# Attention with exponentials on two engines: a third exponential block for VectorE in the first and the third job, and two moved steps

## The chip, the cores and the metric

The kernel runs on one core of a Trainium2 chip. The core has a matrix engine (TensorE, PE in the profile), ScalarE (ACT), VectorE (DVE), GpSimd (POOL) and a queue engine for transfers (SyncE, SP). Each engine carries out its own instruction stream in order; semaphores tell one engine that another has finished something. The metric is the device time of one execution in microseconds. The kernel before takes 412.01 us, the median of three runs (411.99 to 412.39).

## The reference

Grouped-query attention with 8 batches, 512 positions, 32 query heads, 8 key/value heads and head width 64, all in float32:

```python
K_expanded = np.repeat(K, heads_per_group, axis=2)
V_expanded = np.repeat(V, heads_per_group, axis=2)
...
scores = np.einsum('bhqd,bhkd->bhqk', Q, K_expanded) * scale
weights = np.exp(scores - np.max(scores, axis=-1, keepdims=True))
weights = weights / (np.sum(weights, axis=-1, keepdims=True) + 1e-10)

output = np.einsum('bhqk,bhkd->bhqd', weights, V_expanded)
```

There is no mask. Four query heads share one key/value head.

## The kernel before

**Units and jobs.** A unit `u` is one batch and two key/value heads, so there are 32 units. A job `j` is one key/value head of a unit with its four query heads, so there are 64 jobs, and unit `u` has the jobs `2u` and `2u + 1`. A job's four heads form two pairs `i`. For each pair the scores are computed transposed, keys on the 128 partitions and the 512 queries along a row, in four chunks of keys `kc` and for the two heads `m` of the pair. One (i, kc, m) is a block of 128 x 512 scores, and a job has 16 of them.

**Two ways to take an exponential.** Most blocks go to ScalarE, two blocks (1024 columns) to an instruction: `act_tile` (L273) computes the scores on TensorE into a PSUM tile `s_ps` and takes the exponential into `pt` (L279). `s_ps` has two buffers. The first blocks of the second pair, `taken(j)` of them (L242), go another way, by a formula on the bits of a float16 number that VectorE and GpSimd share. `exp_d` (L283) computes their scores into a PSUM tile `d_ps` and scales them to an integer `u` on VectorE (L290). `exp_d2` (L297) takes the mantissa bits `f` on VectorE (L301), then `g` and the product `w` on GpSimd (L304, L308). `exp_d4` (L314) adds `u` and `w` into `pt` on VectorE (L317), and this runs in the middle of the job behind. `d_ps` has one buffer of two banks, each of 512 columns; the same tile name serves for the transposes of Q.

**How many blocks.** `WIDE` (L41) names the jobs in which `taken` is three: the even jobs from 4 on. In all others but the last it is two. With two, ScalarE has seven tiles of 1024 columns; with three, six and one of 512. In the loop, the 512-column tile of a wide job has its scores in the second bank of a `d_ps` tile (`beside`, L563), while the first bank takes a transposed Q. The functions `apart` (L195) and `trans_q(..., other=...)` (L202) tell the framework that two instructions touch different banks of one tile; where nothing is said, the framework makes the later one wait for the earlier one.

**The rest of a job.** `pv` (L333) multiplies the exponentials by the values, 32 matmuls for a pair in four groups of eight, into a PSUM tile with one buffer; a column of ones beside the values gives the sums. `norm` (L372) takes the reciprocal of the sums (L387) and multiplies (L393), and `store` writes a finished unit out through SP. `trans_q` turns a job's Q by TensorE (L210) and VectorE copies it to `qt` (L214). The keys of unit 0 and 1 are turned by TensorE as well (`first_keys` L172, `first_k` L147); those of later units by transposing transfers on SP (`dma_k` L185).

**The order of work** is written out by hand: the text of the kernel is the order of each engine's stream. A job of the loop (L521 to L585) issues its ScalarE tiles 0 to 6 one after the other and puts between them the values and the normalisation of the job before, the transposes of Q for a later job (two jobs ahead; up to job 2 the loop catches up), and the three steps of the other exponential. Near the end of job `j`, the third block of job `j + 1`, where that is a wide one, is computed into the second bank of the `d_ps` tile (L579). Job 0 is written out in front of the loop (L502 to L518).

**Loads.** GpSimd's queue issues the loads of Q, K and V, which also convert to bfloat16. Job 0 and 1 use the Q of unit 0, job 2 and 3 that of unit 1, job 4 and 5 that of unit 2 ("the third unit"). Units 2 and 3 are loaded at the start of job 1, behind a one-element copy `gate` (L528) that waits for ScalarE's fourth tile of job 0, so that these loads stay behind the first ones.

Of the kernel before, what the change touches and what calls it, by code (L numbers as in the profile page):

```python
# [37 lines left out]
LAST_SUMS = NLAST * 2 * 4  # L38


WIDE = lambda j: j >= 4 and j % 2 == 0  # L41


@with_exitstack
# [23 lines left out]
def fast_path(ctx, tc, Q, K, V, out, flag, ident):  # L68
    nc = tc.nc
# [3 lines left out]
    SC = S // 128  # L73
# [26 lines left out]
    gate = const_pool.tile([1, 1], FP16, name="gate")  # L100
# [31 lines left out]
    def load_q(u, lo=0, hi=2 * HPG):  # L132
        b, gp = divmod(u, GP)
        h0 = gp * 2 * HPG
        if u not in qn:
            qn[u] = qnat_pool.tile([128, SC, 2 * HPG, D], BF16, name="q_nat")
        nc.gpsimd.dma_start(  # L137
            out=qn[u][:, :, lo:hi, :],
            in_=Q[b, :, h0 + lo:h0 + hi, :].rearrange("(sc p) h d -> p sc h d", p=128),
        )  # L140

    def d_tile():
        return d_pool.tile([128, 2, S], FP32, name="d_ps")
# [51 lines left out]
    def apart(this, other):  # L195
        if other is not None:
            tc.declare_no_dep(
                this.ins, other.ins, reason="the two are in different banks of one tile"
            )
        return this  # L200

    def trans_q(j, bank, lo=0, hi=NPAIR, other=None):  # L202
        u, g = divmod(j, 2)
        ps = bank.bitcast(BF16).rearrange("p (i sc c) -> p i sc c", i=NPAIR, sc=SC)
        done = []
        for i in range(lo, hi):
            for sc in range(SC):
                h = g * HPG + 2 * i
                done.append(apart(
                    nc.tensor.transpose(ps[:, i, sc, :], qn[u][:, sc, h:h + 2, :], ident), other  # L210
                ))
        if u not in qt:
            qt[u] = qt_pool.tile([128, 2, NPAIR, S], BF16, name="qt")
        return done, lambda: apart(nc.vector.tensor_copy(  # L214
            out=qt[u][:, g, lo:hi, :], in_=ps[:, lo:hi, :, :].rearrange("p i sc c -> p i (sc c)")
        ), other)
# [3 lines left out]
    def piece(bank, done, read):  # L220
        copy = read()
        for other, written, taken_out in pieces:
            if other != bank:
                for this in done:
                    apart(this, taken_out)
                for before in written:
                    apart(copy, before)
        pieces.append((bank, done, copy))
# [13 lines left out]
    def taken(j):  # L242
        return 1 if j == NJOB - 1 else 3 if WIDE(j) else 2

    def d_block(j):
        return SC * 2 - 2 if j == NJOB - 1 else 0

    def act_tiles(j):
        every = [(i, kc, m) for i in range(NPAIR) for kc in range(SC) for m in range(2)]
        first = DPAIR * SC * 2 + d_block(j)  # L250
        mine = [n for n in range(len(every)) if not first <= n < first + taken(j)]
        groups = [[n for n in mine if n // 2 == h] for h in range(len(every) // 2)]
        return [[every[n] for n in group] for group in groups if group]

    jobs, osb, invs = {}, {}, {}
# [17 lines left out]
    def act_tile(j, n, spare=None):  # L273
        group = act_tiles(j)[n]
        i, kc, lo = group[0]
        ps = s_pool.tile([128, 2, S], FP32, name="s_ps") if spare is None else spare
        for _, _, m in group:
            scores(j, ps[:, m, :], i, kc, m)
        return nc.scalar.activation(  # L279
            out=jobs[j]["pt"][:, i, kc, lo:, :], in_=ps[:, lo:, :], func=EXP, scale=scale  # L280
        )

    def exp_d(j, lo, hi, ps, other=None):  # L283
        st = jobs.setdefault(j, {})
        if "u" not in st:
            for name, dtype in (("u", I16), ("f", I16), ("g", BF16), ("w", BF16)):
                st[name] = dve_pool.tile([128, 3, S], dtype, name=name + "16")[:, 0:taken(j), :]
        for n in range(lo, hi):
            apart(scores(j, ps[:, n - lo, :], DPAIR, *divmod(d_block(j) + n, 2)), other)
        return lambda: nc.vector.tensor_scalar(  # L290
            out=st["u"][:, lo:hi, :], in0=ps[:, 0:hi - lo, :], scalar1=A_U, scalar2=B_U,
            op0=ALU.mult, op1=ALU.add,
        )
# [3 lines left out]
    def exp_d2(j, engine=None):  # L297
        st = jobs[j]
        by_bits = engine is None
        engine = engine or nc.gpsimd  # L300
        nc.vector.tensor_single_scalar(  # L301
            out=st["f"], in_=st["u"], scalar=1023, op=ALU.bitwise_and
        )
        engine.tensor_scalar(  # L304
            out=st["g"], in0=st["f"], scalar1=-EXP_F1, scalar2=EXP_K * 2.0 ** (24 * by_bits),
            op0=ALU.add, op1=ALU.mult,
        )
        product = lambda: engine.tensor_tensor(  # L308
            out=st["w"], in0=st["g"], in1=st["f"].bitcast(FP16) if by_bits else st["f"],
            op=ALU.mult,  # L310
        )
        return product() if by_bits else product
# [20 lines left out]
    def pv(j, i, lo, hi):  # L333
        st = jobs[j]
        u, g = divmod(j, 2)
        b, gp = divmod(u, GP)
        if lo == 0:

            t = d_tile() if (j, i) == (NJOB - 1, 0) else pv_tile()
            t = t.rearrange("p m (qc c) -> p m qc c", qc=SC)  # L340
            st["pv"][i] = t[:, :, :, 0:D + 1]
        order = blocks(j, i)
        for n in range(lo, hi):
            kc, m, qc = order[n]
            nc.tensor.matmul(  # L345
                st["pv"][i][:, m, qc, :],
                st["pt"][:, i, kc, m, qc * 128:(qc + 1) * 128],
                vt[b % 2][:, kc, 2 * gp + g, :],
                start=(n < 2 * SC and qc == 0),
                stop=(n >= len(order) - 2 * SC and qc == SC - 1),  # L350
            )
# [136 lines left out]
    bank = pv_tile()  # L488
# [20 lines left out]
    exp_d(0, 0, 2, d_tile())()  # L509
    act_tile(0, 3)  # L510
    act_tile(0, 4)
    exp_d2(0)
    bank = pv_tile()
    piece(0, *trans_q(1, bank[:, 0, :], 0, 1))
    act_tile(0, 5)
    piece(1, *first_keys(1, bank[:, 1, 0:S // 2]))
    act_tile(0, 6)
# [3 lines left out]
    for j in range(1, NJOB - 1):  # L521
        last = j - 1
        u, g = divmod(j, 2)
        b, gp = divmod(u, GP)
        open_job(j)
        if j == 1:

            nc.gpsimd.tensor_copy(out=gate, in_=jobs[0]["pt"][0:1, 0, SC - 1, 0, 0:1])  # L528
            load_q(2)
            load_q(3)  # L530
        if g == 0 and u >= 1 and u + 3 < NU:
            load_q(u + 3)
        if (gp, g) == (1, 0) and b + 1 < B:
            load_k(b + 1)
        if 3 <= 2 * gp + g < 3 + SC and b + 1 < B:
            load_v(b + 1, chunks=(2 * gp + g - 3,))
        if j == 1:
            dma_k(0, 2)
        if gp == 2 and g == 0 and b + 1 < B:
            dma_k(b + 1)  # L540

        cut = (4, 18) if taken(j) > 2 else (11, 19)
        act_tile(j, 0)
        if j == 1:
            piece(1, *first_k(1, 0, bank[:, 1, S // 2:]))
        exp_d(j, 0, 2, d_tile())()
        act_tile(j, 1)

        if j == 8:
            check_v(0, 0)  # L550
        if g == 1 and 1 < j and b < B - 1:
            check_v(b, gp)
        if 0 <= j - 8 * (B - 1) < SC:
            check_v(B - 1, j - 8 * (B - 1))
        pv(last, 0, 0, 16)
        act_tile(j, 2)
        pv(last, 0, 16, 32)
        norm(last, 0)
        act_tile(j, 3)

        reads = []
        bank = d_tile()
        beside = act_tile(j, 4, bank) if taken(j) > 2 else None  # L563

        ahead = (j + 1,) if j < 2 else (3, 4) if j == 2 else (j + 2,)
        for n, to in enumerate(ahead):
            if to < NJOB:
                reads.append(trans_q(to, bank[:, n, :], other=beside)[1])
        if j == 1:
            reads.append(first_k(1, 1, bank[:, 1, :])[1])  # L570
        exp_d4(last)
        check_sums()
        exp_d2(j)
        copies = [read() for read in reads]
        if taken(j) == 2:
            act_tile(j, 4)
        pv(last, 1, 0, cut[0])
        act_tile(j, 5)
        if taken(j + 1) > 2:  # L579
            exp_d(j + 1, 2, taken(j + 1), bank[:, 1:2, :], copies[0])()  # L580
        pv(last, 1, *cut)
        act_tile(j, 6)
        pv(last, 1, cut[1], 32)
        norm(last, 1)
        del jobs[last]  # L585

    j, last = NJOB - 1, NJOB - 2
# [144 lines left out]
```

## Time and profile before

| what | before |
|---|---|
| median of three runs | 412.01 us (411.99 to 412.39) |
| the profiled execution | 412.64 us, its span 410.9 us |
| ScalarE busy | 401.3 us, 98% |
| TensorE busy | 377.8 us, 92% |
| VectorE busy | 342.7 us, 83% |
| GpSimd busy | 306.0 us, 74% |
| granted TensorE clock | 0.998 |

The span reaches from the first to the last instruction; the time of an execution is about 1.7 us longer. In the rows of the profile, a line such as `L279 ACT ACTIVATE pt<-s_ps 128x1024 ... x419 | 396.7, 1298 | 0.6 <-PE s_ps L261 0.6` names the line of the kernel, engine and operation, output and input with their shapes, how often it ran, the time it was busy and the mean length of one in nanoseconds, and the idle time of the engine in front of it with what ended most of it. In a timeline a row gives start and length in microseconds, and equal instructions that follow each other are one row with their number.

### The profile page before, as it was taken

The numbers are of one execution on the slowest core, as the hardware profiler recorded it, in microseconds if no ns is written. First come the engines' busy times: TensorE is split into PE (matmuls) and PEld (weight loads), VectorE is DVE, ScalarE is ACT, GpSimd is POOL, SyncE is SP. The second block draws the span as 40 slices with busy tenths as digits, with TensorE's granted clock in tenths as the row PEclk, the third lists the DMA queues.
The fourth block names the chain that finished last, engine by engine and source line by source line (L and its number), as shares of the span: only waits on it lengthen the run. The fifth ranks groups of instructions, "written<-read, shape, count | busy, mean of one in ns | idle before, by whom it ended". The sixth has DMA issues, their size and how long they took to land.

```text
span 410.9 us, 13048 instructions
## 1 busy us (share of the span) xinstructions
PE 377.8 (92%) x5666; PEld 232.9 (57%) x5666; DVE 342.7 (83%) x609; ACT 401.3 (98%) x454; POOL 306.0 (74%) x216
## 2 busy tenths in 40 slices
PE   7999999999999999999999999999999999999985
PEld 3565565555555555555655655555555655655553
DVE  4787898888888888888888888888889888998775
ACT  5999999999999999999999999999999999999995
POOL 9868767888679777688777897587776887676562
PEclk9999999999999999999999999999999999999999
DMA  9999974999739996499994999669986799742205
GB/s 152 159 244 165 210 148 135 195 140 219 168 107 229 134 230 157 110 203 114 194 270 77 201 185 218 155 86 221 189 176 155 133 202 197 158 138 104 104 30 183
DMA packets 93294, 67.74 MB, mean 165 GB/s; under 512 B 53296, under 2 KB 76336, under 8 KB 93232
## 3 DMA queue, kind: packets, MB, share of 16 engines
q0 software_dynamic: 55488, 24.91, 52.9%
q1 hardware_dynamic: 36688, 41.56, 36.3%
q8 instruction: 45, 0.74, 0.8%
q10 hardware_dynamic: 1056, 0.39, 0.4%
q14 instruction: 17, 0.14, 0.1%
HBM read 50.33 MB, written 33.55 MB: 204 GB/s over the span
## 4 chain that ended last, share of the span: by engine, by line
ACT 86%; PE 8%; DVE 3%; issue 1%; ACTq 0%; POOL 0%; DVEq 0%
ACT pt L279 86%; PE s_ps L261 5%; PE pv L345 2%; DVE o_sb L393 1%; PE s_ps L476 1%; DVE pt L317 1%; DVE qt L214 0%; DVE u L290 0%; ACTq L279 0%; DVE ok L356 0%; DVE inv_last L387 0%; PE pv L493 0%; PE d_ps L345 0%; DVE inv L387 0%; DVE f L301 0%
## 5 line engine op out<-in xcount | busy, mean ns | idle before, releaser
L279 ACT ACTIVATE pt<-s_ps 128x1024 f16<-128x1024 f32 x419 | 396.7, 1298 | 0.6 <-PE s_ps L261 0.6
L345 PEld LDWEIGHTS <-pt 128*128 128x128 f16 x4096 | 142.2, 98 | 75.7 <-issue 55.6
L345 PE MATMUL pv<-v,pt 128*128 128x65 bf16 x4064 | 179.3, 195 | 0.9 <-DVE o_sb L393 0.7
L261 PE MATMUL s_ps<-qt,kt 64*128 64x512 bf16 x781 | 153.1, 383 | 23.7 <-ACT pt L279 17.2
L308 POOL TENSOR_TENSOR w<-g,f 128x1024 bf16<-128x1024 bf16 (+1 forms) x63 | 163.0, 2587 | 5.3
L304 POOL TENSOR_SCALAR g<-f 128x1024 bf16<-128x1024 int16 (+1 forms) x63 | 78.4, 1245 | 90.9 <-DVE f L301 90.8
L290 DVE TENSOR_SCALAR u<-d_ps 128x1024 int16<-128x1024 f32 (+1 forms) x94 | 97.7, 1039 | 0.5 <-PE d_ps L261 0.5
L261 PEld LDWEIGHTS <-kt 64*128 64x128 bf16 x960 | 55.3, 93 | 66.6 <-issue 37.1
L393 DVE TENSOR_TENSOR o_sb<-pv,inv 128x512 f32<-128x512 f32 x121 | 83.7, 692 | 4.2
L387 DVE RECIPROCAL inv<-pv 128x8 f32<-128x8 f32 x121 | 25.1, 207 | 49.9 <-PE pv L345 49.9
L317 DVE TENSOR_TENSOR pt<-u,w 128x1536 uint16<-128x1536 int16 (+1 forms) x64 | 51.4, 803 | 0.3 <-POOL w L308 0.2
L261 PE MATMUL d_ps<-qt,kt 64*128 64x512 bf16 x179 | 46.0, 375 | 0.1
L214 DVE COPY qt<-d_ps 128x1024 bf16<-128x1024 bf16 x62 | 42.3, 684 | 0.0
L210 PEld LDWEIGHTS <-q_nat 128*128 128x128 bf16 x508 | 28.5, 98 | 20.2 <-issue 20.2
L210 PE MATMUL d_ps<-ident,q_nat 128*128 128x128 bf16 x496 | 38.3, 220 | 0.0
L301 DVE TENSOR_SCALAR f<-u 128x1536 int16<-128x1536 int16 (+1 forms) x64 | 31.2, 487 | 0.0
L122 POOL DMA_DIRECT2D v<-in_V_dram x32 | 29.1, 911 | 0.0
L137 POOL DMA_DIRECT2D q_nat<-in_Q_dram x33 | 27.1, 821 | 0.1
L279 ACT ACTIVATE pt<-d_ps 128x512 f16<-128x512 f32 x30 | 26.8, 894 | 0.0
L232 DVE TENSOR_REDUCE okv<-v 128x1 f32<-128x512 bf16 x32 | 21.6, 676 | 0.0
L261 PE MATMUL s_ps<-qt,kt_first 64*128 64x512 bf16 x56 | 11.1, 386 | 2.5 <-ACT pt L279 2.2
L261 PEld LDWEIGHTS <-kt_first 64*128 64x128 bf16 x64 | 4.1, 93 | 6.1 <-issue 3.7
(54 smaller groups left out, 46.2 us busy)
## 6 DMA issues: line engine op xcount, KB each, us to landing
out_dram<-o_sb SPq DMA_DIRECT2D x31, 1024.0 KB, 7.3
q_nat<-in_Q_dram POOLq DMA_DIRECT2D x31, 512.0 KB, 6.3
k_nat<-in_K_dram POOLq DMA_DIRECT2D x7, 512.0 KB, 8.5
v<-in_V_dram POOLq DMA_DIRECT2D x28, 128.0 KB, 7.0
kt<-kt SPq DMA_DIRECT2D x14, 256.0 KB, 4.5
out_dram<-o_sb SPq DMA_DIRECT2D x3, 256.0 KB, 2.3
kt<-k_nat SPq DMA_TRANSPOSE x32, 6.1
v<-in_V_dram POOLq DMA_DIRECT2D x4, 96.0 KB, 8.0
```

The source lines that it names most:

```text
L122: nc.gpsimd.dma_start(out=vt[b % 2][:, sc, lo:hi, 0:D], in_=V[b, sc * 128:(sc + 1) * 128, lo:hi, :],)
L210: nc.tensor.transpose(ps[:, i, sc, :], qn[u][:, sc, h:h + 2, :], ident), other
L214: return done, lambda: apart(nc.vector.tensor_copy(out=qt[u][:, g, lo:hi, :], in_=ps[:, lo:hi, :, :].rearrange("p i sc c -> p i (sc c)")), ...
L261: return nc.tensor.matmul(ps, keys[64 * m:64 * m + 64, g if u == 0 else g ^ m, kc * 128:(kc + 1) * 128], qt[u][64 * m:64 * m + 64, g, i, : ...
L279: return nc.scalar.activation(out=jobs[j]["pt"][:, i, kc, lo:, :], in_=ps[:, lo:, :], func=EXP, scale=scale)
L290: return lambda: nc.vector.tensor_scalar(out=st["u"][:, lo:hi, :], in0=ps[:, 0:hi - lo, :], scalar1=A_U, scalar2=B_U, op0=ALU.mult, op1=AL ...
L301: nc.vector.tensor_single_scalar(out=st["f"], in_=st["u"], scalar=1023, op=ALU.bitwise_and)
L304: engine.tensor_scalar(out=st["g"], in0=st["f"], scalar1=-EXP_F1, scalar2=EXP_K * 2.0 ** (24 * by_bits), op0=ALU.add, op1=ALU.mult,)
L308: product = lambda: engine.tensor_tensor(out=st["w"], in0=st["g"], in1=st["f"].bitcast(FP16) if by_bits else st["f"], op=ALU.mult,)
L317: nc.vector.tensor_tensor(out=st["pt"][:, DPAIR, :, :, :].rearrange("p kc m q -> p (kc m) q")[:, d_block(j):d_block(j) + n, :].bitcast(U16 ...
L345: nc.tensor.matmul(st["pv"][i][:, m, qc, :], st["pt"][:, i, kc, m, qc * 128:(qc + 1) * 128], vt[b % 2][:, kc, 2 * gp + g, :], start=(n < 2 ...
L393: nc.vector.tensor_tensor(out=osb[u][:, lo:hi, h:h + 2, :].rearrange("p qc m d -> p m qc d"), in0=sums[:, :, lo:hi, 0:D], in1=inv[:, :, lo ...
```

## The change

`WIDE` holds for all even jobs, so jobs 0 and 2 hand three blocks to VectorE and GpSimd instead of two. Job 0 takes its third block's scores into a `d_ps` tile of its own behind ScalarE's fifth tile, and `exp_d2` of job 0 comes one transposing step later. The gate and the load of the third Q unit move in front of it. Job 2's third block is computed at the end of job 1, behind ScalarE's last tile instead of in front of the values, where the loop does it for later jobs. Job 2, now a wide one, uses the second `d_ps` bank for its 512-column tile; so the Q of job 4, which was turned in that bank together with the Q of job 3, is turned there later, behind ScalarE's tile 5.

```diff
-WIDE = lambda j: j >= 4 and j % 2 == 0
+WIDE = lambda j: j % 2 == 0
...
     act_tile(0, 4)
-    exp_d2(0)
+    exp_d(0, 2, taken(0), d_tile())()
+    nc.gpsimd.tensor_copy(out=gate, in_=jobs[0]["pt"][0:1, 0, SC - 1, 0, 0:1])
+    load_q(2)
     bank = pv_tile()
     piece(0, *trans_q(1, bank[:, 0, :], 0, 1))
+    exp_d2(0)
     act_tile(0, 5)
...
         if j == 1:
-
-            nc.gpsimd.tensor_copy(out=gate, in_=jobs[0]["pt"][0:1, 0, SC - 1, 0, 0:1])
-            load_q(2)
             load_q(3)
...
-        ahead = (j + 1,) if j < 2 else (3, 4) if j == 2 else (j + 2,)
+        ahead = (j + 1,) if j < 3 else (j + 2,)
...
         act_tile(j, 5)
-        if taken(j + 1) > 2:
+        if j == 2:
+            trans_q(4, bank[:, 1, :])[1]()
+        if taken(j + 1) > 2 and j > 1:
             exp_d(j + 1, 2, taken(j + 1), bank[:, 1:2, :], copies[0])()
         pv(last, 1, *cut)
         act_tile(j, 6)
+        if j == 1:
+            exp_d(2, 2, taken(2), bank[:, 1:2, :], copies[0])()
         pv(last, 1, cut[1], 32)
```

## The prediction

> **What bounds the kernel now.** I read the page first: the busy shares, the chain that ended last, the costliest groups.
>
> ```profile
> span 410.9 us, 13048 instructions
> PE 377.8 (92%) x5666; PEld 232.9 (57%) x5666; DVE 342.7 (83%) x609; ACT 401.3 (98%) x454; POOL 306.0 (74%) x216
> ...
> ACT 86%; PE 8%; DVE 3%; issue 1%; ACTq 0%; POOL 0%; DVEq 0%
> ...
> L279 ACT ACTIVATE pt<-s_ps 128x1024 f16<-128x1024 f32 x419 | 396.7, 1298 | 0.6 <-PE s_ps L261 0.6
> ```
>
> ScalarE is busy 98% and its exponentials idle 0.6 us in all, so every microsecond taken off ScalarE shows, and every wait put on it shows too. The mean of 1298 ns is not the price of a tile, because neighbours overlap. The price is the distance between ends, which the timeline of ScalarE gives (start, length, instruction):
>
> ```profile
> 6.59 29.56 ACT L279 ACTIVATE pt<-s_ps 128x1024 f16<-128x1024 f32 x32 [0.58 <-PE s_ps L261]
> 35.88 0.77 ACT L279 ACTIVATE pt<-d_ps 128x512 f16<-128x512 f32 x1
> 36.36 12.22 ACT L279 ACTIVATE pt<-s_ps 128x1024 f16<-128x1024 f32 x13
> ```
>
> Ends are at 36.15, 36.65 and 48.58: a 512-column tile costs 0.49, and a 1024-column one (48.58 - 36.65) / 13 = 0.917. The first tile, from idle, takes 1.03; 1.03 + 31 x 0.917 = 29.46, so the 32 tiles contain only 0.10 us of waiting. Next the timelines of VectorE and GpSimd, where the added work goes:
>
> ```profile
> 8.45 1.23 DVE L290 TENSOR_SCALAR u<-d_ps 128x1024 int16<-128x1024 f32 x1 [0.48 <-PE d_ps L261]
> 9.71 0.85 DVE L301 TENSOR_SCALAR f<-u 128x1024 int16<-128x1024 int16 x1
> 10.48 0.40 DVE L214 COPY qt<-pv 128x512 bf16<-128x512 bf16 x1
> ...
> 15.96 0.68 DVE L317 TENSOR_TENSOR pt<-u,w 128x1024 uint16<-128x1024 int16 x1
> 16.56 0.42 DVE L301 TENSOR_SCALAR f<-u 128x1024 int16<-128x1024 int16 x1
> 16.90 0.68 DVE L214 COPY qt<-d_ps 128x1024 bf16<-128x1024 bf16 x1
> 17.50 0.41 DVE L160 COPY kt_first<-d_ps 128x512 bf16<-128x512 bf16 x1
> ...
> 21.56 0.21 DVE L387 RECIPROCAL inv<-pv 128x8 f32<-128x8 f32 x1 [0.80 <-PE pv L345]
> ...
> 23.34 1.28 DVE L214 COPY qt<-d_ps 128x1024 bf16<-128x1024 bf16 x2
> ```
>
> ```profile
> 8.65 1.66 POOL L122 DMA_DIRECT2D v<-in_V_dram  x2
> ...
> 36.58 1.47 POOL L304 TENSOR_SCALAR g<-f 128x1536 bf16<-128x1536 int16 x1 [1.66 <-DVE f L301]
> 38.14 3.10 POOL L308 TENSOR_TENSOR w<-g,f 128x1536 bf16<-128x1536 bf16 x1
> ```
>
> See that VectorE's rows of job 1 (15.96 to 17.91) stand without gaps, and that a three-block `f` at 35.94 to 36.49 (0.55) has its `w` only at 41.24, 4.75 later. TensorE in job 2:
>
> ```profile
> 20.85 0.67 PE L345 MATMUL pv<-v,pt 128*128 128x65 bf16 x16
> 21.45 0.39 PE L261 MATMUL s_ps<-qt,kt_first 64*128 64x512 bf16 x2
> 21.77 1.07 PE L210 MATMUL d_ps<-ident,q_nat 128*128 128x128 bf16 x16
> 22.77 0.39 PE L261 MATMUL s_ps<-qt,kt_first 64*128 64x512 bf16 x2
> ```
>
> **The change part by part.** Jobs count from 0, (2,6) is tile 6 of job 2, times are the trace's own clock. Durations by shape are those of the steady state (`u` 1.22 for two blocks and 0.68 for one, `f` 0.42 and 0.55, exp_d4 0.68 and 0.95 for two and three blocks). Small gaps come from neighbouring rows: ScalarE or VectorE to TensorE 0.05, TensorE to either 0.04, `f` to `g` 0.09, `w` to exp_d4 0.03; queued VectorE work starts 0.08 before its predecessor's end.
>
> *Two blocks leave ScalarE* (jobs 0 and 2): 2 x (0.917 - 0.49) = -0.85.
>
> *Job 0's short tile takes an s_ps buffer.* In later wide jobs it sits in d_ps; here the tile behind it needs the buffer of (0,3), which is read until 6.59 + 1.03 + 3 x 0.917 = 10.37. Scores 10.42 to 10.81, exponential from 10.85, 1.03 from idle: end 11.88. Without the wait 10.37 + 0.49 + 0.917 = 11.78. +0.10. Job 0 ends at 12.79 instead of 13.12.
>
> *Job 0's third block, and what is queued behind it.* d_ps has one buffer, so its scores wait for the first `u` (9.68): matmul 9.73 to 10.10, second `u` (0.68) to 10.82, job 1's Q copy to 11.15, `f` of three blocks 11.07 to 11.62. `w` ends 4.75 later, 16.37 (before: 14.05). exp_d4, 0.95 for three blocks, then ends at 17.35 (before: 16.64), where it had been waiting for nothing. Behind it stand job 1's `f` and the copies of job 2's Q and of the swapped keys, 1.27 in the rows (16.64 to 17.91): 18.62. Now the wait: the change puts job 2's third score block on TensorE behind (1,6), into the half of d_ps that the swapped-key copy reads. TensorE stands until 18.68. Queued behind are that matmul (0.31), 13 value matmuls (0.51) and only then (2,0): scores at 19.50, tile end 19.50 + 0.38 + 0.04 + 1.03 = 20.95. Unhindered it is 12.79 + 8 x 0.917 = 20.13. +0.82.
>
> *The Q load moved ahead of `g` on GpSimd.* Its issue (0.82, the mean of such rows) starts near 10.7, behind the memsets and the gate copy (0.18), and ends before `f` (11.62), so `g` loses nothing in the queue. But `f` may: in the trace `f` took 0.85 instead of 0.42 while GpSimd issued a DMA that had begun 0.25 earlier (9.46). An undisturbed 0.42 ending at 10.56 began at 10.14, 0.68 after that issue. The new `f` meets an issue 0.2 to 0.4 old: a delay of 0.28 to 0.48 by that row, zero if it slips in first. All of it passes down the chain above. I take 0.30, the row being nearly the same meeting; ends kept: 0 and 0.48. The trace does not show the other bound, a gain; none is possible, as `f` cannot start before its `u`.
> The Trainium skill ("SBUF — State Buffer", Who interferes with whom) says of VectorE and GpSimd that whoever issues first holds the shared ports for the whole instruction and the other is fully blocked. By that rule `f` would wait for the whole issue; the row above let it go at 0.68.
>
> *The third Q load in the other queues.* load_q(3) now stands behind the longer `w` (16.4 instead of 14.96), load_q(4) and load_k(1) behind job 1's `w` (about 1 later than 20.28 and 21.09). They are wanted in job 4 and after 30 us; median landing is 6.3 and 8.5. Covered, so 0. SP's queue is unchanged.
>
> *Job 4's Q transposed behind (2,5).* In the first place these eight transposes stood in one batch of 16 (21.77, 1.07), which caused the 0.10 of waiting: -0.10. In the new place no independence of the two banks is declared, and in the built order TensorE's first of them waits for VectorE's copy of job 3's Q, out of the other bank of the same tile. When does that copy end? (2,0)'s scores at 19.50 are followed by the first half of job 1's values, which wait for job 0's normalisation (one pv buffer): second `u` of job 2 from 19.09 to 19.77, reciprocal and product to 20.62. Values from 20.68, (2,2) at 21.28, second half 21.60 to 22.27, reciprocal 22.31. From reciprocal to the end of the first Q copy the rows give 23.34 + 0.68 - 21.56 = 2.46, with `f` at three blocks 0.13 more: 24.90. TensorE goes on at 24.96: eight transposes 0.55, 14 values 0.42, switch 0.13, (2,6) at 26.06, tile end 27.51. Unhindered after 20.95: 5 x 0.917 + 0.49, 26.03. +1.48. Their copy waits for ScalarE's short tile, long done.
>
> *Sum.* -0.85 + 0.10 + 0.82 + 0.30 - 0.10 + 1.48 = +1.75; without the delay of `f` +1.45, with 0.48 +1.93. The second wait is counted from (2,0), so a later `f` moves it along and leaves its size. Nothing later gives the sum back, since ScalarE has no idle time. The profiled execution took 412.64, 1.74 beyond its span; it would become 414.39. The median of the runs is 412.01, 0.63 lower; I forecast there: 413.76, about 413.8.
>
> **The rivals.**
> *A. Faster: TensorE arrives at the moved transposes after the copy.* Then also job 2's start is on time; -0.85 + 0.10 - 0.10, 411.2. For it: ScalarE never waited long on TensorE so far. Against: (2,6) must have scores by 24.6, so the copy must end 1.5 sooner than reckoned. Chance 0.04.
> *B. The first wait only.* If the second could pass, -0.85 + 0.10 - 0.10 + 0.82 + 0.30: 412.3, within 0.2%. Against: the wait is in the program. 0.05.
> *C. The second wait only*, job 0's `w` being in time: 412.6, also within 0.2%. Against: 4.75 from `f` to `w`. 0.03.
> *D. `f` waits out the whole issue, or lateness returns in jobs 3 to 5.* If `f` starts at the end of the issue, 0.82 after 10.7 to 10.9, it is 0.44 to 0.64 late: +1.9 to +2.1, 414.1; one more wait of the first kind's half, 0.4, 414.5. Against the second: job 2's `w` is due at 24.30 + 4.75 = 29.05, while job 3's exp_d4, at 28.90 in the trace, moves past 30.3, and by then VectorE has caught up. 0.18. The whole-issue half of it is the rule of the Trainium skill's page named above.
> *E. Both waits but smaller*, `f` slipping in and VectorE's chain a few tenths shorter: +0.85 to +1.45, 413.2. 0.10.
>
> **How the numbers follow.** The main case has 0.60 (413.4 to 414.0). What a measurement can tell from no change is about 0.2%, 0.82 us. A alone is faster: 0.04; B and C are the same: 0.08; main, D and E are slower: 0.88. The range goes from the lower part of E, 412.9 (A, B and C fall outside, 0.12), to 414.4, which leaves out the end of D (0.05).
>
> **What the changed profile would show.** ScalarE's timeline with a 512 tile from s_ps near 10 us and one from d_ps near 23; a three-block `u` pair in job 0; `f` of job 0 longer than 0.55 (the port) or not; exp_d4 of job 0 starting at `w`'s end near 16.7; idle ScalarE of about 1.1 before (2,0), released by scores, and 1.5 before (2,6); TensorE waiting for L160's copy, then for L214's copy ahead of transposes. I am wrong if either gap is missing, or if ScalarE's gaps go on after job 2.

## The result, and the profile after

The kernel after takes 413.77 us, the median of six runs (413.72 to 413.91), the kernel before 412.09 us beside it (411.99 to 412.39). The ratio is 1.004, with a 95% interval of 1.003 to 1.0049: slower by 0.4%, as forecast (413.8). The profiled execution of after took 413.77 us, its span 412.0.

From the page of the kernel after, the same four lines as were shown of before (span, busy times, chain, ScalarE's largest group):

```profile
span 412.0 us, 13049 instructions
...
PE 377.8 (92%) x5666; PEld 232.0 (56%) x5666; DVE 344.3 (84%) x611; ACT 400.5 (97%) x454; POOL 308.1 (75%) x216
...
ACT 80%; PE 10%; DVE 6%; issue 1%; POOL 1%; ACTq 0%; DVEq 0%
...
L279 ACT ACTIVATE pt<-s_ps 128x1024 f16<-128x1024 f32 x418 | 395.4, 1291 | 2.7 <-PE s_ps L261 2.7
```

ScalarE is busy 0.8 us less than before (400.5 for 401.3), which is what the two blocks were to bring. But its exponentials now idle 2.7 us where they idled 0.6, all of it behind scores from TensorE, and the share of other engines in the chain has grown: ScalarE 80% for 86%, TensorE 10% for 8%, VectorE 6% for 3%. Where the 2.7 us lie is read from ScalarE's timeline of after (start, length, instruction, idle time before it and its releaser):

```profile
6.35 9.91 ACT L279 ACTIVATE pt<-s_ps 128x1024 f16<-128x1024 f32 x11 [0.48 <-PE s_ps L261]
16.45 2.85 ACT L279 ACTIVATE pt<-s_ps 128x1024 f16<-128x1024 f32 x3 [0.19 <-PE s_ps L261]
19.97 3.77 ACT L279 ACTIVATE pt<-s_ps 128x1024 f16<-128x1024 f32 x4 [0.66 <-PE s_ps L261]
23.61 0.62 ACT L279 ACTIVATE pt<-d_ps 128x512 f16<-128x512 f32 x1
24.09 1.06 ACT L279 ACTIVATE pt<-s_ps 128x1024 f16<-128x1024 f32 x1
26.52 11.11 ACT L279 ACTIVATE pt<-s_ps 128x1024 f16<-128x1024 f32 x12 [1.37 <-PE s_ps L261]
```

Before, one row of 32 tiles ran from 6.59 to 36.15. Now the row is cut three times, in front of the tiles (1,4), (2,0) and (2,6). In what follows a *gap* is the distance between the ends of two neighbouring tiles beyond the price of the later one, 0.917 us for 1024 columns and 0.49 for 512. It is 0.11 larger than the idle time in the brackets, because a tile that starts from idle takes 1.03. The three gaps are 0.30, 0.77 and 1.48. Two small ones of 0.10 at (0,5) and 0.05 at (1,0) come with them; the 0.10 that before had at (2,4) is gone. From job 3 on there is none. The balance is 2.70 - 0.10 - 0.85 = +1.75 us.

The span grew by 1.1 only, for two reasons. The first exponential began at 6.59 in the profile of before and at 6.35 in that of after; over all profiles of this study it began between 6.27 and 6.70, with no order by kernel. And in the first profile of before the tiles stood 0.09% further apart from beginning to end, 0.36 us in all. A second profile of before (below) lacks that: from the end of the first tile to the end of the last, after is 1.74 us longer than it. This distance, always against the second profile of before, is called the *balance by the trace*.

### The profile page after: what moved, and what is told of

The parts are those of the page before. It is cut to its first block, busy times and chain, and to the rows that moved or that the text cites. A ratio compares the mean times of both kernels' runs of the same rounds, so it can differ in the third digit from the quotient of the medians.

```text
span 412.0 us, 13049 instructions
## 1 busy us (share of the span) xinstructions
PE 377.8 (92%) x5666; PEld 232.0 (56%) x5666; DVE 344.3 (84%) x611; ACT 400.5 (97%) x454; POOL 308.1 (75%) x216
## 4 chain that ended last, share of the span: by engine, by line
ACT 80%; PE 10%; DVE 6%; issue 1%; POOL 1%; ACTq 0%; DVEq 0%
ACT pt L279 80%; PE s_ps L261 5%; PE pv L345 3%; DVE o_sb L393 1%; DVE pt L317 1%; PE s_ps L476 1%; DVE qt L214 1%; DVE u L290 1%; POOL w L308 1%; DVE f L301 1%; DVE inv L387 0%; POOL g L304 0%; DVE ok L356 0%; PE d_ps L210 0%; PE d_ps L261 0%
## 5 line engine op out<-in xcount | busy, mean ns | idle before, releaser
L308 POOL TENSOR_TENSOR w<-g,f 128x1536 bf16<-128x1536 bf16 (+1 forms) x63 | 164.9, 2617 | 5.2
L304 POOL TENSOR_SCALAR g<-f 128x1536 bf16<-128x1536 int16 (+1 forms) x63 | 79.1, 1256 | 89.9 <-DVE f L301 89.9
L290 DVE TENSOR_SCALAR u<-d_ps 128x1024 int16<-128x1024 f32 (+1 forms) x96 | 99.0, 1031 | 1.4 <-PE d_ps L261 1.4
L317 DVE TENSOR_TENSOR pt<-u,w 128x1536 uint16<-128x1536 int16 x64 | 51.9, 811 | 0.9 <-POOL w L308 0.8
L301 DVE TENSOR_SCALAR f<-u 128x1536 int16<-128x1536 int16 x64 | 31.3, 489 | 0.0
L114 POOL DMA_DIRECT2D k_nat<-in_K_dram x9 | 6.7, 749 | 0.0
```

The source lines that it names most:

```text
L290: return lambda: nc.vector.tensor_scalar(out=st["u"][:, lo:hi, :], in0=ps[:, 0:hi - lo, :], scalar1=A_U, scalar2=B_U, op0=ALU.mult, op1=AL ...
L301: nc.vector.tensor_single_scalar(out=st["f"], in_=st["u"], scalar=1023, op=ALU.bitwise_and)
L304: engine.tensor_scalar(out=st["g"], in0=st["f"], scalar1=-EXP_F1, scalar2=EXP_K * 2.0 ** (24 * by_bits), op0=ALU.add, op1=ALU.mult,)
L308: product = lambda: engine.tensor_tensor(out=st["w"], in0=st["g"], in1=st["f"].bitcast(FP16) if by_bits else st["f"], op=ALU.mult,)
L317: nc.vector.tensor_tensor(out=st["pt"][:, DPAIR, :, :, :].rearrange("p kc m q -> p (kc m) q")[:, d_block(j):d_block(j) + n, :].bitcast(U16 ...
```

## The experiments

The table has each kernel's median, the ratio to the runs of before beside it with its 95% interval, the balance by the trace, and the sum of its own terms: -0.43 for each block that leaves ScalarE, the gaps, and -0.10 where the gap at (2,4) is gone.

| run | median, us | ratio | balance by the trace | sum of the terms |
|---|---|---|---|---|
| before again | 412.24 | 1.0006 (0.9976 to 1.0036) | 0 | 0 |
| after again | 413.80 | 1.0038 (1.0018 to 1.0059) | +1.81 | +1.81 |
| e1, banks declared apart | 413.16 | 1.0004 (0.9977 to 1.003) | +0.78 | +0.79 |
| e2, load back in job 1 | 413.83 | 1.0011 (0.9983 to 1.004) | +1.54 | +1.55 |
| e3, job 2's block only | 412.90 | 0.9996 (0.9971 to 1.002) | +0.74 | +0.73 |
| e4, job 0's block only | 412.14 | 0.9995 (0.997 to 1.002) | +0.32 | +0.33 |
| e5, copies first | 413.04 | 1.0015 (0.9993 to 1.0037) | +0.99 | +1.00 |
| e9, job 4's Q behind (2,6) | 412.62 | 1.0015 (1.0 to 1.003) | +0.44 | +0.42 |
| e14, job 2's block, Q behind (2,6) | 411.69 | 0.999 (0.9981 to 0.9999) | -0.43 | -0.46 |
| e18, every wait treated | 411.75 | 0.9988 (0.9976 to 1.0) | -0.12 | -0.14 |
| e19, e18 with the K load moved | 413.08 | 1.0018 (0.9994 to 1.0043) | +0.79 | +0.76 |

The last two columns agree within 0.04 us in all rows, so ScalarE's gaps account for the whole balance. Both columns come from the same row of tiles: their agreement shows that no gap was missed, and what made each gap is left to the comparisons below. The medians carry more: the start of the first exponential, and runs of before from 411.94 to 417.39. A difference of a few tenths is therefore read from the trace, not from two medians. The waits that the gaps belong to are told apart next.

### The two kernels again

> The kernel before as it is, for a second profile. Theory: one gap, of 0.10 in job 2, and none else, with a distance of 0.917 between the ends of tiles that differs by under 0.1% from the first profile's; the 0.2 to 0.3 by which the first exponential starts earlier or later, seen between the profiles so far, belongs to the first loads and not to a kernel.

> The changed kernel as it is, on the same chip and beside the same runs of the kernel before. Theory: gaps of 0.10, 0.05, 0.30, 0.77 and 1.48 again, 1.6 to 1.7 above before.

The timeline of ScalarE in the second profile of before is one row as in the first:

```profile
6.63 29.54 ACT L279 ACTIVATE pt<-s_ps 128x1024 f16<-128x1024 f32 x32 [0.62 <-PE s_ps L261]
```

It has the single gap of 0.10 at (2,4). After has its gaps again: 0.10, 0.12, 0.30, 0.76 and 1.48.

### e1: the banks of job 4's Q and job 3's Q declared apart

```diff
         if j == 2:
-            trans_q(4, bank[:, 1, :])[1]()
+            turned, read = trans_q(4, bank[:, 1, :])
+            for this in turned:
+                apart(this, copies[0])
+            read()
```

> The changed kernel with one declaration more: the transposes of job 4's Q are told to lie in another bank than the one VectorE copies job 3's Q from. Theory (the wait in front of the moved transposes is one between two banks): the transposes then wait only for ScalarE's short tile, which really is read from their bank and ends at 24.23, instead of the copy, which let them go at 25.11. They start near 24.28, 0.83 earlier, and all of it reaches tile (2,6): its gap falls from 1.48 to about 0.65, the time from 413.8 to about 412.95. Rival (TensorE's own work or VectorE's chain sets (2,6), and the wait on the copy only fills time that would be lost anyway): 413.8, gap unchanged. Second rival (nothing else is waited for): gap gone, 412.3.

The gap at (2,6) is 0.65 for 1.48, and (2,0) stays at 0.77. The gap at (1,4) is 0.20 for 0.30 and that at (1,0) is gone, which is not the work of the edit and is taken up under e2. TensorE at the transposes, in after and then in e1:

```profile
22.80 0.62 PE L210 MATMUL d_ps<-ident,q_nat 128*128 128x128 bf16 x8
...
23.59 0.39 PE L261 MATMUL s_ps<-qt,kt_first 64*128 64x512 bf16 x2
25.11 0.61 PE L210 MATMUL d_ps<-ident,q_nat 128*128 128x128 bf16 x8 [1.14 <-DVE qt L214]
25.56 0.60 PE L345 MATMUL pv<-v,pt 128*128 128x65 bf16 x14
26.09 0.39 PE L261 MATMUL s_ps<-qt,kt_first 64*128 64x512 bf16 x2
```

```profile
24.29 0.61 PE L210 MATMUL d_ps<-ident,q_nat 128*128 128x128 bf16 x8 [0.30 <-ACT pt L279]
24.74 0.60 PE L345 MATMUL pv<-v,pt 128*128 128x65 bf16 x14
25.27 0.39 PE L261 MATMUL s_ps<-qt,kt_first 64*128 64x512 bf16 x2
```

In after, TensorE stands 1.14 us for VectorE's copy of job 3's Q, although that copy reads the other bank of the tile. In e1 it stands 0.30, and now for ScalarE's 512-column tile (23.63 to 24.25), the true user of the bank. So 0.83 of the largest gap was a wait between two banks that share nothing but a tile name. What is left of it, 0.65, is the wait for the bank itself, and the eight transposes and 14 values in front of (2,6).

### e2: the third Q load back at the start of job 1

```diff
     exp_d(0, 2, taken(0), d_tile())()
-    nc.gpsimd.tensor_copy(out=gate, in_=jobs[0]["pt"][0:1, 0, SC - 1, 0, 0:1])
-    load_q(2)
...
         if j == 1:
+            nc.gpsimd.tensor_copy(out=gate, in_=jobs[0]["pt"][0:1, 0, SC - 1, 0, 0:1])
+            load_q(2)
             load_q(3)
```

> The changed kernel with the gate copy and the load of the third Q unit back at the start of job 1. Theory (f of job 0 is drawn out by the transfer that GpSimd issues beside it): f takes 0.55 instead of 0.84, everything behind it comes 0.28 earlier, the gap of 0.30 in front of tile (1,4) nearly goes and the 0.77 before (2,0) stays: about 413.45. Rival (three blocks simply take f that long there, or the gap at (1,4) is TensorE's own work): f at 0.84 or the gap unchanged, 413.8. Rival (the load was moved because it is late otherwise): a wait for Q in job 2, over 413.8.

Job 0's `f` on VectorE, in after and then in e2:

```profile
10.84 0.84 DVE L301 TENSOR_SCALAR f<-u 128x1536 int16<-128x1536 int16 x1
```

```profile
10.75 0.55 DVE L301 TENSOR_SCALAR f<-u 128x1536 int16<-128x1536 int16 x1
```

Without a GpSimd issue beside it, `f` takes the 0.55 that three blocks take elsewhere. The gap at (1,4) falls from 0.30 to 0.07 and the one at (1,0) is gone; (2,0) stays at 0.76 and (2,6) at 1.48, and 0.09 appears at (3,0). The balance is +1.54 for +1.74. The delay of `f` thus cost 0.28 at two places, and 0.09 came back. The median, 413.83, doesn't show the 0.2 us; for the time alone this run decides nothing.

Runs that keep the load in job 0 show the same by degrees. In e1 and e9 the first exponential began at 6.49 and 6.48 instead of 6.35, so `f` met the issue later and took 0.64 and 0.63. The gaps at (1,0) and (1,4) together are 0.07 with `f` at 0.55 (e2), 0.20 and 0.19 with 0.64 and 0.63 (e1, e9), 0.35 with 0.84 (after) and 0.42 with 0.90 (after again).

### e3 and e4: one of the two blocks alone

e3 leaves job 0 at two blocks:

```diff
-WIDE = lambda j: j % 2 == 0
+WIDE = lambda j: j >= 2 and j % 2 == 0
...
-    exp_d(0, 2, taken(0), d_tile())()
```

> The changed kernel with three blocks in job 2 alone; job 0 hands over two as before, all else as changed. Theory (two separate waits): the first gap (before (2,0), and the 0.30 before (1,4)) is gone, the second stays at 1.2 to 1.5 since it depends on the bank and not on the first. -0.43 for the block, -0.10 for the batch of 16 transposes split up, +1.2 to 1.5: 412.1 + 0.7 to 0.97 = 412.8 to 413.1. Rival (the second gap is a consequence of TensorE being late from the first): both gone, 411.6.

e4 leaves job 2 as it was before:

```diff
-WIDE = lambda j: j % 2 == 0
+WIDE = lambda j: j % 2 == 0 and j != 2
...
-        ahead = (j + 1,) if j < 3 else (j + 2,)
+        ahead = (j + 1,) if j < 2 else (3, 4) if j == 2 else (j + 2,)
...
-        if j == 2:
-            trans_q(4, bank[:, 1, :])[1]()
...
-        if j == 1:
-            exp_d(2, 2, taken(2), bank[:, 1:2, :], copies[0])()
```

> The changed kernel with three blocks in job 0 alone; job 2 hands over two, with its Q transposes in one batch as before. Theory (the 0.77 before (2,0) comes from job 2's third block, which waits for the copy of the swapped keys and has the values of job 0 behind it): without that block (2,0) is on time, while the waits of job 0's own block stay, 0.10 behind the short tile and 0.35 before (1,0) and (1,4). -0.43 + 0.10 + 0.35 = +0.02: 412.1, the same as before. Rival (the late w and exp_d4 of job 0 hold (2,0) back by themselves): +0.77 more, 412.9.

In e3 ScalarE's timeline has one cut, in front of (2,6), with a gap of 1.26; (2,0) has none, so `w` of job 0 is in time when it has two blocks. The wait at (2,6) is 0.22 shorter than in after: the copy of job 3's Q ends as long after the scores of (2,0) begin (18.60 to 24.03, in after 19.54 to 24.96), but here these scores lie ready before ScalarE needs them. So the second wait depends somewhat on the first.

```profile
25.59 4.69 ACT L279 ACTIVATE pt<-s_ps 128x1024 f16<-128x1024 f32 x5 [1.15 <-PE s_ps L261]
```

In e4 (2,0) and (2,6) have none, and 0.20, 0.05 and 0.30 stand at (0,5), (1,0) and (1,4). So the wait at (2,0) needs both blocks: job 0's makes `w` late, and job 2's puts a matmul behind that lateness. The wait at (1,4) comes from job 0's part alone. The gap at (0,5) is 0.20 where after has 0.10. One gap was not expected at all, 0.205 at (4,0). TensorE's row there, and in the view of the keys' tile `kt` the line of what its engine waited for (us, times):

```profile
31.39 0.88 PE L261 MATMUL s_ps<-qt,kt 64*128 64x512 bf16 x2
```

```profile
  DMA kt<-kt: 0.5, 1
```

The first matmul runs, the second waits half a microsecond for a transfer, the swapped keys of unit 2. They landed at 31.3 and 31.8 us in e4, and at 29.9 and 30.7 in before. In after they were as late (31.5 and 31.8), but ScalarE was later too and nothing waited. What makes them late stays open: e3, with the third Q load at the same place, had them at 30.5 and 30.7.

### e5: in job 1 the copies ahead of exp_d4

```diff
-        cut = (4, 18) if taken(j) > 2 else (11, 19)
+        cut = (4, 18) if taken(j) > 2 else (11, 16) if j == 1 else (11, 19)
...
+        if j == 1:
+            copies = [read() for read in reads]
         exp_d4(last)
...
         exp_d2(j)
-        copies = [read() for read in reads]
+        if j != 1:
+            copies = [read() for read in reads]
```

> The changed kernel with another order in job 1 alone: VectorE copies job 2's Q and the swapped keys before the late exp_d4 of job 0 instead of behind it, and TensorE does three of the value matmuls that need exp_d4 behind tile (1,6) instead of in front of it. Theory (the first gap is VectorE's queue: the key copy stands behind exp_d4, which waits for w): the copies end near 17, job 2's third block is not held, the 0.77 before (2,0) goes; the 0.35 before (1,0) and (1,4), made by f, stays, and so does the second gap, 1.35 to 1.5. 413.8 - 0.77 - 0 to 0.1 = about 413.0. Rival (exp_d4 itself, wanted by the values of job 0, is what TensorE waits for): gap before (2,0) unchanged in size, 413.8.

VectorE in the middle of job 1, in after and then in e5:

```profile
16.45 0.96 DVE L317 TENSOR_TENSOR pt<-u,w 128x1536 uint16<-128x1536 int16 x1 [0.61 <-POOL w L308]
17.32 0.42 DVE L301 TENSOR_SCALAR f<-u 128x1024 int16<-128x1024 int16 x1
17.66 0.69 DVE L214 COPY qt<-d_ps 128x1024 bf16<-128x1024 bf16 x1
18.26 0.42 DVE L160 COPY kt_first<-d_ps 128x512 bf16<-128x512 bf16 x1
```

```profile
16.11 0.69 DVE L214 COPY qt<-d_ps 128x1024 bf16<-128x1024 bf16 x1 [0.29 <-PE d_ps L155]
16.72 0.41 DVE L160 COPY kt_first<-d_ps 128x512 bf16<-128x512 bf16 x1
17.05 0.95 DVE L317 TENSOR_TENSOR pt<-u,w 128x1536 uint16<-128x1536 int16 x1
```

The copy of the swapped keys ends at 17.13 in place of 18.68, and the gap at (2,0) is gone; (1,4) stays at 0.30 and (2,6) at 1.47. The balance falls from +1.74 to +0.99, by the size of that gap. The edit also moves three value matmuls behind (1,6), which was not tried alone. That `w` is late costs ScalarE nothing by itself: it costs what stands behind it on VectorE and holds `d_ps`.

### e9: job 4's Q turned behind tile (2,6)

```diff
         act_tile(j, 5)
-        if j == 2:
-            trans_q(4, bank[:, 1, :])[1]()
...
         act_tile(j, 6)
+        if j == 2:
+            turned, read = trans_q(4, bank[:, 1, :])
+            for this in turned:
+                apart(this, copies[0])
+            read()
```

> The changed kernel with the transposes of job 4's Q behind tile (2,6) instead of behind (2,5), and the two banks declared independent. Theory (it is the place that costs: in front of (2,6) the bank is not free, first because of the copy from the other bank, then because of ScalarE's short tile): the 1.48 before (2,6) goes, some 0.1 to 0.3 comes back before (3,0), where TensorE has eight transposes more; the first gaps stay. 413.8 - 1.48 + 0.2 = 412.5. Rival (the transposes only carry the wait with them, into job 3): gap of over 1 before (3,0), 413.3 or more.

The row of ScalarE now goes through (2,6), and the cut comes in front of (3,0):

```profile
24.08 1.98 ACT L279 ACTIVATE pt<-s_ps 128x1024 f16<-128x1024 f32 x2
26.24 4.72 ACT L279 ACTIVATE pt<-s_ps 128x1024 f16<-128x1024 f32 x5 [0.18 <-ACT pt L279]
```

The gap there is 0.29, so of the 1.48 at (2,6) the order and the declaration together recover 1.19, against 0.83 for the declaration alone (e1). The order without the declaration was not run; in e9 the transposes begin at 24.76, before the copy out of the other bank ends (24.95), so the declaration is used there too.

### e14: job 2's block alone, its transposes behind (2,6)

This joins e3 and e9, the load staying ahead of `g`.

```diff
-WIDE = lambda j: j % 2 == 0
+WIDE = lambda j: j >= 2 and j % 2 == 0
...
-    exp_d(0, 2, taken(0), d_tile())()
...
         act_tile(j, 5)
-        if j == 2:
-            trans_q(4, bank[:, 1, :])[1]()
...
         act_tile(j, 6)
+        if j == 2:
+            turned, read = trans_q(4, bank[:, 1, :])
+            for this in turned:
+                apart(this, copies[0])
+            read()
```

> Three blocks in job 2 alone (job 0 two, as before), and the transposes of job 4's Q behind (2,6) with the banks declared independent. Theory: no gap of job 0's block, none before (2,6). -0.43 for the block, -0.10 for the batch of transposes, +0.03 to 0.1 before (3,0): -0.45, 411.6 where before is 412.1, if the swapped keys of unit 2, which land near 30.7, are still in time for (4,0). Rival (another wait comes up as ScalarE runs ahead, in (4,0) above all): same as before, 412.1.

ScalarE's timeline:

```profile
6.70 16.61 ACT L279 ACTIVATE pt<-s_ps 128x1024 f16<-128x1024 f32 x18 [0.69 <-PE s_ps L261]
23.10 0.69 ACT L279 ACTIVATE pt<-d_ps 128x512 f16<-128x512 f32 x1
23.58 12.22 ACT L279 ACTIVATE pt<-s_ps 128x1024 f16<-128x1024 f32 x13
```

No cut is left; a gap of 0.07 remains at (3,0). The median is 411.69 us, 0.6 below that of before beside it, the ratio 0.999 (0.9981 to 0.9999). It is the one kernel of the study whose interval lies below 1, and only just; the trace is the firmer ground. By it the kernel gains 0.43, the price of one half tile.

### e18 and e19: both blocks, with every wait treated

e18 takes e5 and e9 together, puts job 0's short tile into the second bank of its third block's `d_ps` tile, loads the third Q unit right behind the first values, and loads the keys of the next batch a job later.

```diff
     load_v(0, 2, KV)
-    nc.gpsimd.memset(ones, 1.0)
-    nc.gpsimd.memset(ok, 1.0)
+    load_q(2)
...
-    act_tile(0, 4)
-    exp_d(0, 2, taken(0), d_tile())()
-    nc.gpsimd.tensor_copy(out=gate, in_=jobs[0]["pt"][0:1, 0, SC - 1, 0, 0:1])
-    load_q(2)
+    both = d_tile()
+    short = act_tile(0, 4, both)
+    apart(exp_d(0, 2, taken(0), both[:, 0:1, :], short)(), short)
...
     exp_d2(0)
+    nc.gpsimd.memset(ones, 1.0)
+    nc.gpsimd.memset(ok, 1.0)
...
-        if (gp, g) == (1, 0) and b + 1 < B:
+        if (gp, g) == ((1, 1) if b == 0 else (1, 0)) and b + 1 < B:
             load_k(b + 1)
```

> Both blocks moved and every wait found taken away: job 0's short tile in the second bank of the d_ps tile of its third block; the third Q unit loaded right behind the first V loads, so that the transfer is issued before f; in job 1 the copies before exp_d4 and fewer values before (1,6); job 4's Q transposed behind (2,6); and the second batch's K loaded a job later, so that it does not compete with the copies of unit 2's swapped keys, for which job 4 waited 0.2 in an earlier run. Theory (the gaps found are all there is): -0.85 for the blocks, -0.10 for the batch, +0.07 before (1,4), +0.16 before (3,0): -0.7, 411.4 where before is 412.1. Rival (ScalarE ahead of the rest finds the next late thing, a transfer or TensorE's own work in jobs 1 to 4): gaps of 0.3 or more at new places, 411.8 to 412.3.

e19 is e18 with the load of the next batch's keys between `g` and `w` of job 2:

```diff
         )
+        if j == 2:
+            load_k(1)
         product = lambda: engine.tensor_tensor(
...
-        if (gp, g) == ((1, 1) if b == 0 else (1, 0)) and b + 1 < B:
+        if (gp, g) == (1, 0) and 0 < b < B - 1:
```

> The kernel with both blocks moved and all found waits taken away, in which the second batch's K had come so late that job 8 waited 0.34 for its transposed keys. Here that K is loaded between g and w of job 2, some 3 us earlier, still behind the copies of unit 2's swapped keys. Theory: no gap before (4,0) and none before (8,0), -0.34 against the former: 411.4 where before is 412.1. Rival (the load competes with the swapped keys again, or w of job 2 comes late by the 0.75 of the issue): a gap before (4,0) or in job 3, 411.7 or more.

In e18 the gaps up to job 6 are 0.06, 0.23 and 0.18, so the balance stood at -0.46 there, no better than e14 with half the blocks. Then (8,0) waits 0.34 for the keys that the moved load brings, as TensorE's row shows:

```profile
56.27 0.39 PE L261 MATMUL s_ps<-qt,kt 64*128 64x512 bf16 x1 [0.25 <-DMA kt<-kt]
```

Its time, 411.75, is level with e14's; it gained less than was expected. In e19 that wait is gone, but the beginning is worse: the gaps are 0.27, 0.63 and 0.16 at (0,4) to (0,6), 0.16 at (1,0) and 0.30 at (1,4), and 0.18 at (3,0) as in e18. Here are three stretches of e19 and then the first two of them in e18 (length; busy time of PE, PEld, DVE, ACT and POOL with counts; granted TensorE clock, DMA share, GB/s):

```profile
6.98:10.39 3.41, 1.88 (x15) 0.75 (x14) 2.62 (x4) 3.41 (x4) 3.41 (x6) 1.00 1.37 182
10.39:13.80 3.41, 3.41 (x20) 1.34 (x18) 2.34 (x5) 2.67 (x4) 2.13 (x2) 0.50 1.79 162
13.80:17.20 3.40, 3.40 (x58) 2.15 (x58) 2.38 (x4) 3.34 (x5) 3.39 (x4) 1.00 1.74 187
```

```profile
6.98:10.39 3.41, 2.24 (x17) 0.81 (x15) 2.43 (x4) 3.41 (x5) 3.41 (x6) 1.00 1.43 196
10.39:13.80 3.41, 3.02 (x40) 1.62 (x38) 2.93 (x7) 3.41 (x5) 2.85 (x3) 1.00 1.97 165
```

From 10.39 to 13.80 TensorE was granted half its clock, where e18 has all of it, and it got through 20 matmuls for 40. TensorE's rows of e19 show where it began:

```profile
10.18 0.46 PE L261 MATMUL d_ps<-qt,kt_first 64*128 64x512 bf16 x2 [1.10 <-DVE u L290]
10.57 0.61 PE L210 MATMUL pv<-ident,q_nat 128*128 128x128 bf16 x4
11.11 0.61 PE L261 MATMUL s_ps<-qt,kt_first 64*128 64x512 bf16 x2
```

After 1.10 us of waiting a pair of score matmuls takes 0.61 in place of 0.39. The runs of e19 spread from 411.50 to 414.51, so a median of it says little of its order of work. e18 has the same order in job 0, stood 0.75 at the same place and kept its clock. The first gap, at (0,4), comes with the wait itself; those at (0,5) and (0,6) stand inside the slow stretch. That the longer wait lowers the clock was not tried by itself and stays open. So does the best place for the keys' load.

## Why the prediction was right, point by point

Counted from the start of the first exponential (6.59 in the profile that the prediction worked from, 6.35 in that of after), the steps fell so. The 0.30 for `f` is added to the prediction's times, as its text asks.

| step | predicted | measured |
|---|---|---|
| `f` of job 0 ends | 11.92 - 6.59 = 5.33 | 11.68 - 6.35 = 5.33 |
| `w` of job 0 ends | 16.67 - 6.59 = 10.08 | 16.41 - 6.35 = 10.06 |
| swapped-key copy ends | 18.92 - 6.59 = 12.33 | 18.68 - 6.35 = 12.33 |
| tile (2,0) ends | 21.25 - 6.59 = 14.66 | 20.99 - 6.35 = 14.64 |
| copy of job 3's Q ends | 25.20 - 6.59 = 18.61 | 24.96 - 6.35 = 18.61 |
| tile (2,6) ends | 27.81 - 6.59 = 21.22 | 27.54 - 6.35 = 21.19 |

**Two blocks leave ScalarE, -0.85.** Right: ScalarE's busy time fell by 0.8, and every row of the table of experiments adds up with 0.43 a block.

**Job 0's short tile in `s_ps`, +0.10.** Right in size: 0.10 at (0,5). That the buffer alone makes it is not shown. In front of these scores TensorE also has the third block, which waits for the first `u`; e18, where the short tile takes no `s_ps` buffer, keeps 0.06 there, and e4 has 0.20.

**Job 0's third block and the queue behind it, +0.82.** Right in size and cause. In e2, where `f` is undisturbed, the terms are 0.07 and 0.76. e3 has no such gap because `w` is early, e4 has none because nothing stands behind it, and e5 removes it by taking the copies out from behind exp_d4. TensorE's rows of after show the wait itself, and the scores of (2,0) behind it:

```profile
18.73 0.37 PE L261 MATMUL d_ps<-qt,kt_first 64*128 64x512 bf16 x1 [0.68 <-DVE kt_first L160]
19.04 0.57 PE L345 MATMUL pv<-v,pt 128*128 128x65 bf16 x13
19.54 0.39 PE L261 MATMUL s_ps<-qt,kt_first 64*128 64x512 bf16 x2
```

**The Q load ahead of `g`, +0.30.** The size came out: `f` took 0.84 in place of 0.55. Luck had a part in it. The prediction had the issue at 10.7 and `f` ready at 11.07. In after they were at 10.55 and 10.84, because the first exponential began 0.24 earlier than in the profile it worked from; `f` held to the same instant, 11.12, but ready at 11.08, would have lost some 0.04 (an estimate). The runs gave 0.07 (e9) to 0.35 (after again), all between the bounds of 0 and 0.48 that it kept. The sentence that failed is "All of it passes down the chain above": by that the gap at (2,0) should have been 0.82 + 0.30 = 1.12. It was 0.77, and ScalarE had already lost 0.05 at (1,0) and 0.30 at (1,4); the sum, 1.12, is the same. The step had followed `f` only through GpSimd to `w`. Behind `f` on VectorE stands the copy of the keys for (1,0) as well, and TensorE waited for it. TensorE's rows of after, here and in front of (1,4):

```profile
12.06 0.39 PE L261 MATMUL s_ps<-qt,kt_first 64*128 64x512 bf16 x2 [0.51 <-DVE kt_first L181]
...
15.12 0.62 PE L210 MATMUL d_ps<-ident,q_nat 128*128 128x128 bf16 x8
15.67 0.41 PE L155 MATMUL d_ps<-ident,k_nat 128*64 128x128 bf16 x8
16.02 0.39 PE L261 MATMUL s_ps<-qt,kt_first 64*128 64x512 bf16 x2
```

The 16 transposes in front of (1,4) leave TensorE no slack to make up a late start. That this batch is the link between the two is read from the rows, not shown by a run; that the gap goes with `f`'s delay is shown by e2, and that it belongs to job 0's part by e4. The loss at (2,0) is counted from the end of job 1, so what was lost at (1,4) was not lost a second time. The sum came out right because both ways end at the same instant.

**The other queues, 0.** Right for after, where no transfer is waited for, and without margin: in e4, where ScalarE is less late, the swapped keys cost 0.2. The prediction's "covered" spoke of the Q and K loads and had not looked at the swapped keys, which SP issues at about 24 us and which landed less than 1 us ahead of use in before.

**Job 4's Q behind (2,5), +1.48 and -0.10.** Right: 1.48 at (2,6), and the gap at (2,4) is gone. e1 shows that the wait for the other bank is 0.83 of it, and e9 that 0.29 is left when the transposes stand behind (2,6). The size is not quite free of the first wait: with (2,0) on time it is 1.26 in e3. In e5, also with (2,0) on time, it is 1.47; there job 2's `f` (22.92) met another GpSimd issue (22.44) and took 0.66 instead of 0.55.

**The sum, +1.75 for 1.68.** The medians are 1.68 apart, the balance by the trace is 1.74. The two large waits and their causes are shown by runs; that the sum agrees to a hundredth owes something to the luck with `f`: e1 and e9, with `f` held less, lost 0.15 less in job 1. The rivals: A (411.2) fell, since both waits are there; B and C fell, since neither wait is alone; e9 and e5, which each take one of them away, show that the other then costs 412.62 and 413.04. D fell, since `f` was held 0.29 us, where the whole row of the issue (10.55 to 11.32) would have made it 0.48, and job 3 has no gap. E fell with the delay of `f`.

## What to carry to other kernels

Here, where one engine was busy 98% of the time, the gain of the work taken off it could be reckoned to a tenth of a microsecond; what decides is what each new step stands behind in the queues of the engines that feed it. Follow an instruction that becomes late through everything queued behind it on its own engine, not only through its result. Declare the independence of two banks that share a tile name, and put a moved step behind the last instruction that the bound engine needs soon: here both together turned one block from +0.7 into -0.4 us.

## What the runs showed of the hardware

**A GpSimd DMA issue holds VectorE's `f` for a part of itself.** Where the issue began first, `f` behaves as if it had begun 0.17 to 0.20 us before the end of the issue's row. In after the row lasts from 10.55 to 11.32, and `f`'s end less its own 0.555 is 11.12. The same holds in after again, e1, e4, e5, e9 and e18, and in both profiles of before for a two-block `f` of 0.42. Counted from the start of the issue it is 0.56 to 0.59 where the row lasts 0.77, and 0.66 to 0.68 where it lasts 0.83 to 0.85. Where `f` began first it took its plain time, as in e14, VectorE's and then GpSimd's timeline:

```profile
10.70 0.42 DVE L301 TENSOR_SCALAR f<-u 128x1024 int16<-128x1024 int16 x1
```

```profile
10.77 0.77 POOL L137 DMA_DIRECT2D q_nat<-in_Q_dram  x1
```

The Trainium skill ("SBUF — State Buffer", Who interferes with whom) says that whichever of VectorE and GpSimd issues first holds the shared ports for the whole instruction. For VectorE first, `f`'s plain 0.42 in e14 agrees; a block of GpSimd does not show there, since the issue's row is as short as in after (0.77) though `f` ran beside it for 0.35. For GpSimd first, the hold measured in after ends 0.2 us ahead of the end of the issue's row (0.57 of 0.77), so the rule gives 0.2 too much there.

**TensorE's clock can fall inside the first 20 us of an execution.** In e19 it was granted 0.50 from 10.39 to 13.80 us, and 1.00 before and after. In the 3.41 us in front TensorE was busy for 1.88, with an idle time of 1.10; in the same stretch of the other twelve profiles it was busy for 2.24 to 2.66 and kept its clock.

The Trainium skill ("TensorE: Matmul & The Clock Gate", Part 1) has the clock fall to half after about 3.4 us of idling. The half agrees with e19; the idling does not, since 1.10 us was the longest idle time in the stretch. No run here shows how little work is enough.

**The swapped keys' landing varied by more than their margin.** The two transfers of the third unit's swapped keys, issued by SP, landed at 29.9 and 30.7 us in before and at 30.2 and 30.9 in before again. With the third Q loaded in job 0 they landed at 30.5 and 30.7 in e3, at 31.3 and 31.8 in e4, and in the two profiles of after at 31.5 and 31.8, and at 29.8 and 32.2. In e2, with that load back in job 1, it was 32.1 and 32.5. They were earliest in e18, at 28.8 and 29.1, where SP issued them at 22.6 instead of 24.1 in before. So the place of the Q load alone does not order them; the cause stays open.
